# A hybrid decoder layer on one core: query blocks of three head groups multiplied in pairs by seven half products, attention's tasks ranked ahead, and the meta tokens' small copies moved from POOL to ACT

## The chip, the cores and the metric

The kernel runs on one core of a Trainium2 chip. The metric is the device time of one execution in microseconds (us); lower is better. Engines: PE multiplies matrices, DVE and ACT work on vectors and read and write SBUF and PSUM, POOL (GpSimd) does small vector work in SBUF, and SP starts the transfers. Every engine works through its own instructions in a fixed order.

## The reference, cut to what matters

A layer with two branches on the same normalised input `hn` (16 meta tokens and 512 tokens, 1024 wide), all in float32:

```python
proj = hn @ w_in.astype(h.dtype)
aq, ak, av, az, dq, dk, dv, dz, db, da, ga, gd = jnp.split(proj, offs, axis=-1)
o_a = diff_attention(qa, ka, va, lam)
y_a = (o_a * jax.nn.silu(az)) @ w_branch_attn.astype(h.dtype)
qkv = jnp.concatenate([dq, dk, dv], axis=-1)
qkv = jax.nn.silu(causal_depthwise_conv(qkv, conv_w))
o_d = gated_delta_chunked(pad_front(q), pad_front(k), pad_front(v), pad_front(beta), pad_front(g))
y_d = (o_d * jax.nn.silu(dz)) @ w_branch_delta.astype(h.dtype)
merged = jax.nn.sigmoid(ga) * y_a + jax.nn.sigmoid(gd) * y_d
return merged @ w_out.astype(h.dtype)
```

Attention has 8 heads with two softmax maps each, of which the second is subtracted with the weight `lam`. The delta rule has 8 heads of 128; its queries, keys and values (`dq`, `dk`, `dv`) pass a causal convolution over four tokens. It solves a triangular system in each chunk and carries a state from chunk to chunk. The output is normalised and the meta tokens are dropped.

## The kernel before, in words

**Blocks.** The columns of `w_in` are cut into blocks of 128, one per head and kind (`dq 3`, `av 5`). `dense_order` lists them in the order in which PE multiplies them. Heads go in four groups of two. In groups one to three the order is: both `dk`, both `dv`; then `ak av aq az` of the first attention head; both `dq`; one `dz`; `ak av aq az` of the second head; the other `dz`. Group nought has another order. The gate blocks `gd` and `ga` and the branches' products `yd` and `ya` come after the groups.

**Weights.** Each product is made in three passes: high part by high part, high by low, low by high (`PASSES`, the lists `hnH`, `hnL`, `wh`, `wl`). A raw block arrives by DMA in one of four buffers `raw`; ACT casts it to `wh`, and DVE writes `wl = raw - wh`. There are three buffers for such a pair of parts (`W`).

**Two ways to multiply.** `product` takes one block alone: 8 slices of the inner dimension by three passes, for each of two pieces of the tokens. For `dq` the pieces have 258 columns (`QSEG`; the first 12 tokens aren't needed). Its result goes by `conv_silu`, where ACT copies two pieces from PSUM into a buffer `xp`, into the convolution `conv`. `pair_of_blocks` multiplies two neighbouring blocks together. The two blocks, the two halves of the inner dimension and the two halves of the tokens (264 columns each) make eight half products; with sums of the weights (`split_pair`: four sums of 128x512 on DVE in `raw` and `st`, then four pairs of high and low parts, `wa`, `wb`, `wc` of 1024 columns and `wd` of 512) and sums of the tokens (`sumH`, `sumL`, made once) seven are enough. The parts of the result are put together afterwards: ACT copies the running sum three times (`snap`, `snap_c`, one of them into the single buffer `cn`), and DVE makes four totals of 128x264 straight into `xp` (or `vT` for attention). Then `whole_dk` or `whole_dv` runs the same `conv`. Before the change `dk` and `dv` of groups one to three and all `ak av` are multiplied in pairs.

**The order of the work** is made by a planner (`Plan`) when the kernel is built. Each task is a generator that yields the engine, the event or the buffer it wants next. At every step the planner takes the task that can begin first by its own cost figures; when several can begin at the same time, which on a busy engine is nearly always so, the lower `rank` goes first, and buffers are given out by rank too. Delta tasks have rank 0, the steps after a product rank 1, attention 2, the products 4. A helper emits all instructions, so that all have line 231 in the profile; they are told apart by their tiles.

**The delta rule of a group** (`delta_pair`): `keys` transposes the keys and `products` multiplies them; `queries` makes `qT` by `kT` and scales `qT`; the triangular recursion is 31 steps of two small DVE instructions on `tmps` and `ts`; `steps` then runs the chunks. The meta tokens are treated apart: the first 16 columns of the two heads' keys and values are copied into `km` and `vm` (POOL, a copy of 128x16 for each head), and PE transposes `km` and `vm`. In `meta_tokens` a power on POOL (`ms`) scales the transposed values to `vrm`.

**Attention** (`attention`, one task per head): scores into PSUM `psc`, the row maximum in `ast`, exponentials `e` on ACT; `combine` takes the reciprocal of a row sum, multiplies it by `nlam` and by `l0` to the scale of the second map, and puts the two maps together.

Of the kernel before, what the change touches and what calls it, by code (L numbers as in the profile page):

```python
# [21 lines left out]
NM = 16  # L22
# [34 lines left out]

ORDER = dense_order()

PAIRS = [n for n, (name, i) in enumerate(ORDER) if name == "ak" or name in ("dk", "dv") and i > 1 and i % 2 == 0]  # L60
PAIRED = {m for n in PAIRS for m in (n, n + 1)}
HALF = L // 2
PASSES = ((0, 0), (0, 1), (1, 0))
# [25 lines left out]
class Plan:  # L89
# [24 lines left out]
    def spawn(self, gen, rank=None):  # L114
        time, src = self.here() if self.task else (0.0, SP)
        self.tasks.append(Task(gen, self.task.rank if rank is None else rank, time, src))

    def done(self, event):
        self.events[event] = self.here()
# [146 lines left out]
def hybrid_block(ctx: ExitStack, tc: tile.TileContext, x, meta, wblk, wbd, wout, pcol, prow, out):  # L266
# [630 lines left out]
    def whole_dv(h, which):  # L897
        pair["v", h], _ = yield from conv(which, 16 + h, 0, None)
        done(f"dv{h}")

    def after_dq(h, banks):
        pair["q", h], _ = yield from conv_silu(banks, h, NM, "qT")
        give("y")
        done(f"dq{h}")
# [82 lines left out]
    def delta_pair(gi):  # L987
# [41 lines left out]
        def keys(i):  # L1029
            h = hs[i]  # L1030
            yield f"dk{h}"
            k = pair["k", h]

            def head():
                yield POOL
                G.tensor_copy(out=km[:, 16 * i:16 * i + 16], in_=k[:, 0:NM])
                tick(name("km"), 2)

            spawn(head())
            yield ("ktd",)  # L1040
            kd[i] = slot(dp, [P, NC, P], F32, "ktd")
            t4 = sc[:, i, :, :]
            yield ("pdl",)
            yield PE
            pt = bank("pdl").rearrange("p (c d) -> p c d", d=P)
            for c in range(NC):
                T.transpose(pt[:, c, :], k[:, chunk(c)], ident)
            for c in range(NC):
                yield ACT
                A.activation(out=mk(dp, [P, P], F32, "sqk", 1), in_=pt[:, c, :], func=AF.Square,  # L1050
                             accum_out=t4[:, c, kt_:kt_ + 1])

            def decayed():

                for c in range(NC):
                    yield ACT
                    A.activation(out=kd[i][:, c, :], in_=pt[:, c, :], func=AF.Copy, scale=edl[:, c, h:h + 1])
                give("pdl", pt)
                done(f"kd{h}")

            spawn(decayed())
            yield DVE
            V.tensor_scalar_add(out=t4[:, :, kt_], in0=t4[:, :, kt_], scalar1=4e-6)

            def root():
                yield DVE
                V.tensor_scalar_mul(out=t4[:, :, vs_], in0=t4[:, :, kt_], scalar1=0.25)
                yield POOL
                G.tensor_tensor(out=t4[:, :, vs_], in0=t4[:, :, vs_], in1=phalf[:, 0:4], op=ALU.pow)
                done(f"vs{h}")  # L1070

            spawn(root())
            yield DVE
            V.reciprocal(out=t4[:, :, s_], in_=t4[:, :, kt_])
            yield DVE
            V.tensor_tensor(out=t4[:, :, s_], in0=t4[:, :, s_], in1=beta[:, 0:4, h], op=ALU.mult)
            done(f"s{h}")

        def values(i):
            h = hs[i]  # L1080
            yield f"dv{h}"
            v = pair["v", h]
            yield POOL
            G.tensor_copy(out=vm[:, 16 * i:16 * i + 16], in_=v[:, 0:NM])
            tick(name("vm"), 2)
            yield ("vr",)
            vr[i] = slot(dp, [P, NC, P], F32, "vr")
            yield f"vs{h}"
            yield ("pdl",)
            yield PE  # L1090
            pt = bank("pdl").rearrange("p (c d) -> p c d", d=P)
            for c in range(NC):
                T.transpose(pt[:, c, :], v[:, chunk(c)], ident)
            give("y")
            for c in range(NC):
                yield ACT
                A.activation(out=vr[i][:, c, :], in_=pt[:, c, :], func=AF.Copy, scale=sc[:, i, c, vs_:vs_ + 1])
            give("pdl", pt)
            done(f"v{h}")
# [413 lines left out]
    def attention(h):  # L1513
# [11 lines left out]
        def combine(i, st, es):  # L1525
            N = NM + P * (i + 1)
            yield DVE
            V.reciprocal(out=st[:, 5:6], in_=st[:, 4:5])
            yield DVE
            V.scalar_tensor_tensor(out=st[:, 6:7], in0=st[:, 5:6], scalar=nlam, in1=l0[:, i:i + 1], op0=ALU.mult, op1=ALU.mult)  # L1530
            yield DVE
            V.scalar_tensor_tensor(out=es[0], in0=es[1], scalar=st[:, 6:7], in1=es[0], op0=ALU.mult, op1=ALU.add)
            give("e")

            yield ("pm",)
            which = plan.task.slot
            pm = late["pm"][which]
            yield ACT
            A.copy(out=pm[:, 0:2, 0:NM], in_=es[0][:, 0:NM].unsqueeze(1).broadcast_to([P, 2, NM]))
            yield DVE  # L1540
            V.tensor_tensor(out=pm[:, 2, 0:NM], in0=es[0][:, 0:NM], in1=pm[:, 0, 0:NM].bitcast(F32), op=ALU.subtract)
            yield ("pT",)
            pT, pmT = slot(ap, [P, NC, P], F32, "pT"), mk(ap, [96, P], F32R, "pmT", SLOTS["pT"])
            yield ("pat",)
            yield PE
            pt = bank("pat")
            for n in range(i + 1):
                T.transpose(pt[:, n * P:(n + 1) * P], es[0][:, chunk(n)], ident)
            give("e")
            w = (i + 1) * P  # L1550
            dst = pT[:, 0:i + 1, :].rearrange("p n q -> p (n q)")
            yield ACT
            A.copy(out=dst, in_=pt[:, :w])
            give("pat", pt)
            yield ("pat",)
            po = bank("pat")
            yield PE
            T.transpose(po[0:96, P:2 * P], pm.rearrange("p a t -> p (a t)").bitcast(F32), ident)
            plan.give("pm", which)
            yield ACT  # L1560
            A.copy(out=pmT, in_=po[0:96, P:2 * P])
            yield PE
            T.matmul(po[:, 0:P], pmT, late["vm"], start=True, stop=False)
            for n in range(i + 1):
                T.matmul(po[:, 0:P], pT[:, n, :], vs[:, n, :], start=False, stop=n == i)
            give("pT")
            yield ACT
            A.copy(out=o[:, i, :], in_=po[:, 0:P])
            A.activation(out=po[:, P:2 * P], in_=po[:, 0:P], func=AF.Square, accum_out=ss[:, i:i + 1])
            give("pat", po)  # L1570
            tick(f"ao{h}", NC)
# [71 lines left out]
    tails, highs, lows = dict(od=[None] * H, oa=[None] * H), {}, {}  # L1643

    AFTER = dict(dk=after_dk, dv=after_dv, dq=after_dq, aq=after_aq)
    WHOLE = dict(dk=whole_dk, dv=whole_dv, ak=whole_ak, av=whole_av)
    parts, th_, mg = {}, {}, {}

    def branch(name, of):
# [499 lines left out]
    for n, rank in ((1, 0), (0, 0.1), (2, 0.2), (3, 0.4), (4, 0.5)):  # L2149
        spawn(normalise(n), rank)  # L2150
    for h in range(H):
        spawn(attention(h), 2)
    plan.run()


# [44 lines left out]
```

## Time and profile before

| | before |
|---|---|
| median of 3 runs | 757.09 us (756.8 to 757.27) |
| the profiled execution's own time | 757.23 us |
| its span, first to last instruction | 755.5 us |
| PE busy | 734.0 us, 97% of the span |
| PEld busy (loading of weights into PE) | 666.7 us, 88% |
| DVE busy | 624.5 us, 83% |
| ACT busy | 495.8 us, 66% |
| POOL busy | 84.4 us, 11% |
| granted PE clock | 0.998 of full speed |

The profile is one execution. A group row gives an instruction's form, its count, busy time and mean duration in ns, then the idle time just before it and what ended that. A timeline row begins with the start and the duration in us; in square brackets stands the idle time before it and what released it. A row of waits gives the total, the number and the longest. Matmuls overlap, so the duration of one is longer than its share of PE's time.

### The profile page before, as it was taken

To read this page: it belongs to the slowest core of one execution; us is meant where nothing else is said; L and a number is where in the kernel's file an instruction comes from. 1 tells how busy PE (TensorE), PEld (TensorE's weight loads), DVE (VectorE), ACT (ScalarE), POOL (GpSimd) and SP (SyncE) were. 2 spreads that over 40 slices of the span, in tenths; PEclk is the share of its full clock that TensorE was granted. 3 is DMA by queue.
4 is the path that set the end of the run, shared out by engine and by line. 5 is a ranking of instruction groups with operands and counts; after the bars stand their busy time and mean duration, and the time that the engine had idled before them with its cause. 6 is when DMAs were issued, how large, how long until landed. Compare 5 with 4: busy or idle time off the path is not lost.

```text
span 755.5 us, 14375 instructions
## 1 busy us (share of the span) xinstructions
PE 734.0 (97%) x5311; PEld 666.7 (88%) x5311; DVE 624.5 (83%) x1431; ACT 495.8 (66%) x1306; POOL 84.4 (11%) x102
## 2 busy tenths in 40 slices
PE   4999999999999999999999999999999999999996
PEld 4998988989899899999889989988988998899875
DVE  6999999978899779989978989984697869797453
ACT  6369565869875778985587986767776445555132
POOL 3216000203000202200020300100100000000001
PEclk9999999999999999999999999999999999999999
DMA  8141322315304122531320441361023443132602
GB/s 307 52 135 33 111 82 66 92 29 155 113 29 153 18 70 85 168 85 43 120 65 29 150 138 37 125 184 58 29 83 113 142 130 121 56 119 90 240 4 108
DMA packets 45430, 74.86 MB, mean 99 GB/s; under 512 B 20728, under 2 KB 25636, under 8 KB 45360
## 3 DMA queue, kind: packets, MB, share of 16 engines
q1 hardware_dynamic: 45360, 73.95, 31.2%
q8 instruction: 41, 0.67, 0.4%
q14 instruction: 29, 0.24, 0.1%
HBM read 67.58 MB, written 6.36 MB: 98 GB/s over the span
## 4 chain that ended last, share of the span: by engine, by line
PE 81%; DVE 7%; ACT 5%; issue 2%; POOL 2%; DMA 1%; SPq 0%; POOLq 0%; ACTq 0%; DVEq 0%
PE bank L231 78%; PE psc L231 3%; DVE wl L231 2%; DVE y L231 1%; ACT wh L231 1%; POOL ms L231 1%; DMA xt<-in_x_dram 1%; ACT ak L231 1%; ACT sqk L231 0%; DVE aq L231 0%; DMA odd<-room 0%; ACT TM L231 0%; DVE room L231 0%; DVE hnL L231 0%; POOL ass L231 0%
## 5 line engine op out<-in xcount | busy, mean ns | idle before, releaser
L231 PE MATMUL bank<-hnH,wh 128*128 128x512 f32 (+4 forms) x664 | 232.7, 354 | 1.1 <-ACT hnH L231 0.8
L231 PE MATMUL bank<-hnH,wl 128*128 128x512 f32 (+4 forms) x664 | 221.6, 337 | 0.0
L231 PE MATMUL bank<-hnL,wh 128*128 128x512 f32 (+4 forms) x664 | 221.5, 337 | 0.0
L231 ACT CAST wh<-raw 128x1024 fp32r<-128x1024 f32 (+1 forms) x120 | 116.4, 971 | 48.8 <-PE bank L231 43.8
L231 DVE TENSOR_TENSOR wl<-raw,wh 128x1024 fp32r<-128x1024 f32 (+1 forms) x120 | 134.8, 1124 | 13.1 <-ACT wh L231 12.6
L231 PEld LDWEIGHTS bank<-hnH,wh 128*128 128x128 f32 x664 | 124.4, 189 | 14.7 <-ACT hnH L231 1.0
L231 PEld LDWEIGHTS bank<-hnH,wl 128*128 128x128 f32 x664 | 124.1, 188 | 14.0
L231 PEld LDWEIGHTS bank<-hnL,wh 128*128 128x128 f32 x664 | 124.4, 189 | 9.0
L231 PE MATMUL bank<-sumH,wh 128*128 128x264 f32 x224 | 67.3, 300 | 0.0
L231 PE MATMUL bank<-sumH,wl 128*128 128x264 f32 x224 | 63.5, 284 | 0.0
L231 PE MATMUL bank<-sumL,wh 128*128 128x264 f32 x224 | 63.5, 284 | 0.0
L231 DVE SCALAR_TENSOR_TENSOR y<-xp,pc,y 128x528 f32<-128x528 f32 (+1 forms) x72 | 54.5, 759 | 1.3 <-ACT y L231 1.2
L231 PEld LDWEIGHTS bank<-sumH,wh 128*128 128x128 f32 x224 | 42.3, 189 | 0.6 <-issue 0.2
L231 PEld LDWEIGHTS bank<-sumL,wh 128*128 128x128 f32 x224 | 42.3, 189 | 0.0
L231 PEld LDWEIGHTS bank<-sumH,wl 128*128 128x128 f32 x224 | 42.1, 188 | 0.0
L231 ACT ACTIVATE e<-psc,ast 128x144 f32<-128x144 f32 (+3 forms) x64 | 34.5, 541 | 8.7 <-DVE ast L231 8.2
L231 PE MATMUL bank<-btH,wh 128*128 128x256 f32 x128 | 36.2, 283 | 0.5 <-ACT sn L231 0.5
L231 PE MATMUL bank<-btH,wl 128*128 128x256 f32 x128 | 35.9, 280 | 0.0
L231 PE MATMUL bank<-btL,wh 128*128 128x256 f32 x128 | 35.9, 280 | 0.0
L231 ACT CAST wh<-st 128x1024 fp32r<-128x1024 f32 x22 | 23.1, 1048 | 16.2 <-PE bank L231 15.9
L231 POOL TENSOR_TENSOR ass<-ass,mhalf 128x4 f32<-128x4 f32 x8 | 8.7, 1084 | 222.8 <-DVE ass L231 163.4
L231 DVE TENSOR_TENSOR wl<-st,wh 128x1024 fp32r<-128x1024 f32 x22 | 27.8, 1266 | 2.4 <-ACT wh L231 2.3
(373 smaller groups left out, 1732.3 us busy)
## 6 DMA issues: line engine op xcount, KB each, us to landing
raw<-in_wblk_dram SPq DMA_DIRECT2D x96, 512.0 KB, 3.5
raw<-in_wout_dram SPq DMA_DIRECT2D x8, 512.0 KB, 4.9
xt<-in_x_dram SPq DMA_DIRECT2D x4, 512.0 KB, 6.2
TM<-gcd SPq DMA_DIRECT2D x8, 256.0 KB, 5.4
xr<-in_x_dram SPq DMA_DIRECT2D x8, 256.0 KB, 6.4
out_dram<-xr SPq DMA_DIRECT2D x8, 256.0 KB, 2.2
room<-scrm SPq DMA_DIRECT2D x12, 128.0 KB, 3.4
oad<-room SPq DMA_DIRECT2D x6, 256.0 KB, 3.8
```

Source lines behind the costliest of these rows:

```text
L231: return real(*args, **kw)
```

## The change

- `PAIRS` takes in `dq` of groups one to three: those six blocks are multiplied as three pairs by seven half products. A new function `whole_dq` runs the convolution on a finished block, as `whole_dk` does.
- The copies into `km` and `vm` go from POOL to ACT.
- The scale of attention's second map is made by a `tensor_scalar` with two column scalars on `l0`, where a `scalar_tensor_tensor` stood; the product is the same.
- Attention's tasks get rank 1 where they had 2.

```diff
-PAIRS = [n for n, (name, i) in enumerate(ORDER) if name == "ak" or name in ("dk", "dv") and i > 1 and i % 2 == 0]
+PAIRS = [n for n, (name, i) in enumerate(ORDER) if name == "ak" or name in ("dk", "dv", "dq") and i > 1 and i % 2 == 0]
...
+    def whole_dq(h, which):
+        pair["q", h], _ = yield from conv(which, h, NM, "qT")
+        give("y")
+        done(f"dq{h}")
...
-                yield POOL
-                G.tensor_copy(out=km[:, 16 * i:16 * i + 16], in_=k[:, 0:NM])
+                yield ACT
+                A.copy(out=km[:, 16 * i:16 * i + 16], in_=k[:, 0:NM])
...
-            yield POOL
-            G.tensor_copy(out=vm[:, 16 * i:16 * i + 16], in_=v[:, 0:NM])
+            yield ACT
+            A.copy(out=vm[:, 16 * i:16 * i + 16], in_=v[:, 0:NM])
...
-            V.scalar_tensor_tensor(out=st[:, 6:7], in0=st[:, 5:6], scalar=nlam, in1=l0[:, i:i + 1], op0=ALU.mult, op1=ALU.mult)
+            V.tensor_scalar(out=st[:, 6:7], in0=l0[:, i:i + 1], scalar1=st[:, 5:6], scalar2=nlam, op0=ALU.mult, op1=ALU.mult)
...
-    WHOLE = dict(dk=whole_dk, dv=whole_dv, ak=whole_ak, av=whole_av)
+    WHOLE = dict(dk=whole_dk, dv=whole_dv, dq=whole_dq, ak=whole_ak, av=whole_av)
...
-        spawn(attention(h), 2)
+        spawn(attention(h), 1)
```

In the instruction lists of the engines the change shows as follows. PE, group one, the query blocks before the change, where the first block's second piece ends and the second block's first piece begins (`wh_21` and `wl_22` are the first block's parts, `wh_23` and `wl_24` the second's):

```order
L231 MATMUL bank_5_82<-hnH,wh_21_118 128x258
L231 MATMUL bank_5_82<-hnL,wh_21_118 128x258
L231 MATMUL bank_5_82<-hnH,wl_22_119 128x258
L231 MATMUL bank_3_80<-hnH,wh_23_120 128x258
L231 MATMUL bank_3_80<-hnL,wh_23_120 128x258
L231 MATMUL bank_3_80<-hnH,wl_24_121 128x258
```

And after it, in the middle of the pair's seven products, where one half product with token sums ends and the next, with the same weights' other half, begins (`sumH`, `sumL` are the token sums' high and low parts):

```order
L231 MATMUL bank_4_81<-sumH_37_136,wh_23_120 128x264
L231 MATMUL bank_4_81<-sumL_41_140,wh_23_120 128x264
L231 MATMUL bank_4_81<-sumH_37_136,wl_24_121 128x264
L231 MATMUL bank_6_83<-sumH_34_133,wh_23_120 128x264
L231 MATMUL bank_6_83<-sumL_38_137,wh_23_120 128x264
L231 MATMUL bank_6_83<-sumH_34_133,wl_24_121 128x264
```

In each of the three groups 96 products of 258 columns become 84 of 264; PE has 36 products fewer in all, and nothing else is added to it or taken from it.

DVE, group one, before: the sums of the second attention pair (`st`, `raw`), and the first two instructions of the triangular recursion (`tmps`, `ts`) among them:

```order
L231 TENSOR_TENSOR st_115<-raw_14_111 128x512
L231 TENSOR_TENSOR st_115<-st_115,raw_16_113 128x512
L231 TENSOR_TENSOR wl_20_117<-raw_17_114,wh_19_116 128x1024
L231 TENSOR_TENSOR raw_14_111<-raw_16_113,raw_14_111 128x512
L231 TENSOR_TENSOR ak_2563<-vT_93_655,ak_2563 64x528
L231 SCALAR_TENSOR_TENSOR aq_2564<-bank_2_79,aq_2564 64x512
L231 TENSOR_TENSOR tmps_2602<-room_31_130,ts_1613 99x31
L231 SCALAR_TENSOR_TENSOR room_32_131<-room_33_132,bank_4_81 128x512
L231 TENSOR_TENSOR ts_1613<-ts_1613,tmps_2602 99x31
```

After, ahead of that place: the new sums of the query pair, among the low parts of other blocks and the meta tokens' scales (`ms`):

```order
L231 TENSOR_TENSOR st_115<-raw_15_112 128x512
L231 TENSOR_TENSOR wl_20_117<-raw_16_113,wh_19_116 128x1024
L231 TENSOR_TENSOR vT_93_655<-bank_6_83,vT_93_655 128x264
L231 TENSOR_TENSOR st_115<-st_115,raw_14_111 128x512
L231 TENSOR_TENSOR ms_952<-ms_952,medl 32x1
L231 TENSOR_TENSOR wl_22_119<-raw_14_111,wh_21_118 128x1024
L231 TENSOR_TENSOR raw_15_112<-raw_14_111,raw_15_112 128x512
L231 TENSOR_SCALAR ms_952<-blk_103,ms_952 32x2
L231 TENSOR_TENSOR raw_14_111<-raw_14_111,st_115 128x512
```

The query pair's four sums stand ahead of group one's recursion, whose first instruction now comes 37 rows behind the last of them; the sums of the second attention pair come behind that first instruction.

POOL, group nought, as a piece of the difference (`km` and `vm` are the meta tokens' columns, `ms` the power, `TM` the decay masks):

```order
-L231 COPY km_668<-kT_549 128x16
-L231 COPY km_668<-kT_604 128x16
-L231 COPY vm_669<-y_612 128x16
 L231 TENSOR_TENSOR sc_665<-sc_665,phalf 128x4 x2
 L231 TENSOR_TENSOR ms_670<-ms_670,phalf 32x1
-L231 AFFINE_SELECT TM_680<-TM_680 128x512
-L231 COPY vm_669<-y_797 128x16
-L231 AFFINE_SELECT TM_680<-TM_680 128x512
+L231 AFFINE_SELECT TM_680<-TM_680 128x512 x2
```

The four copies leave POOL's list; the last of them stood behind the power `ms` and a mask. On ACT that last copy now stands right behind the second of the four casts of token sums (`sumH`).

## The prediction

> **What bounds the kernel now.** I read the page first: its busy times, and the chain of work that ended last.
>
> ```profile
> span 755.5 us, 14375 instructions
> PE 734.0 (97%) x5311; PEld 666.7 (88%) x5311; DVE 624.5 (83%) x1431; ACT 495.8 (66%) x1306; POOL 84.4 (11%) x102
> PE 81%; DVE 7%; ACT 5%; issue 2%; POOL 2%; DMA 1%; SPq 0%; POOLq 0%; ACTq 0%; DVEq 0%
> ```
>
> PE is occupied for 734 of 755.5 us and carries 81% of the chain. So a product that PE no longer makes is worth its time, if the others keep PE fed. Second, PE's waits, longest first:
>
> ```profile
> PE bank L231 <- ACT st L231: 7.7, 1, 7.7
> PE bank L231 <- POOL vm L231: 1.7, 1, 1.7
> PE bank L231 <- DVE ss L231: 1.3, 2, 0.9
> PE bank L231 <- ACT hnH L231: 0.8, 1, 0.8
> PE bank L231 <- DVE tdmt L231: 0.6, 1, 0.6
> ```
>
> The first, third and fourth belong to the start, which the change does not touch. Behind the start only one wait is longer than 0.6 us: that for `vm` on POOL.
>
> Third, busy time by stage. The first three rows are the stretches from a group's query products to the end of its triangular recursion; the fourth is the stage from 125 to 500 us, in which the three changed groups lie; the last three come just ahead of the query products.
>
> ```profile
> 205.00:250.00 45.00, 45.00 (x315) 41.47 (x314) 43.51 (x127) 29.65 (x82) 1.01 (x1) 1.00 0.25 77
> 330.00:375.00 45.00, 44.72 (x316) 41.50 (x315) 43.83 (x127) 28.78 (x79) 1.58 (x1) 1.00 0.27 86
> 455.00:500.00 45.00, 45.00 (x320) 41.82 (x319) 43.64 (x128) 30.82 (x85) 2.20 (x3) 1.00 0.36 115
> 125.00:500.00 375.00, 372.09 (x2913) 343.21 (x2912) 331.34 (x830) 284.94 (x841) 49.77 (x62) 1.00 0.31 92
> ...
> 195.00:205.00 10.00, 10.00 (x66) 8.74 (x65) 7.48 (x19) 7.15 (x26) 0.00 (x0) 1.00 0.39 107
> 320.00:330.00 10.00, 10.00 (x61) 8.68 (x61) 6.38 (x18) 7.00 (x24) 0.00 (x0) 1.00 0.24 67
> 450.00:455.00 5.00, 5.00 (x34) 4.48 (x34) 2.09 (x5) 2.19 (x10) 0.00 (x0) 1.00 0.67 189
> ```
>
> The columns after the length are PE, PEld, DVE, ACT, POOL, the clock and DMA. From 125 to 500 us PE idles for 2.9 us. DVE, which writes the low parts of the weights, is idle for 1.5, 1.2 and 1.4 us of each 45 us stretch: 97% busy. Ahead of the query products it idles for 2.5, 3.6 and 2.9 us. So PE is the bound, and DVE is second just where the change adds work to it.
>
> How thin is the cover? In the timeline I looked for each low part's end on DVE and its first use on PE. It is thinnest at the attention query block that follows the group's second pair of attention blocks:
>
> ```profile
> 360.69 1.22 DVE L231 TENSOR_TENSOR wl<-raw,wh 128x1024 fp32r<-128x1024 f32 x1
> 485.53 1.22 DVE L231 TENSOR_TENSOR wl<-raw,wh 128x1024 fp32r<-128x1024 f32 x1
> ```
>
> ```profile
> 364.65 0.40 PE L231 MATMUL bank<-hnH,wl 128*128 128x512 f32 x1
> 489.17 0.39 PE L231 MATMUL bank<-hnH,wl 128*128 128x512 f32 x1
> ```
>
> The weights are ready at 361.91 and 486.75 and used at 364.65 and 489.17: 2.7 and 2.4 us ahead, 2.6 in the mean.
>
> **The change part by part: PE.** Two query blocks take 2 x 2 x 8 x 3 = 96 products of 258 columns now. As a pair they take 7 x 4 x 3 = 84 of 264 columns. The duration of one (0.28 us) is not its price, since the next starts earlier; I take start to start, from the first and last row of two unbroken stretches, of 39 and 56 products:
>
> ```profile
> 51.06 0.28 PE L231 MATMUL bank<-hnH,wh 128*128 128x258 f32 x1
> ...
> 55.61 0.28 PE L231 MATMUL bank<-hnH,wl 128*128 128x258 f32 x1
> ...
> 130.39 0.29 PE L231 MATMUL bank<-hnL,wh 128*128 128x264 f32 x1
> ...
> 137.06 0.28 PE L231 MATMUL bank<-sumH,wl 128*128 128x264 f32 x1
> ```
>
> (55.61 - 51.06) / 38 = 0.1197 us, and (137.06 - 130.39) / 55 = 0.1213 us. A pair saves 96 x 0.1197 - 84 x 0.1213 = 11.49 - 10.19 = 1.30 us, three pairs 3.9 us. The wider columns are paid in this; the seven half products remove an eighth of the products, not an eighth of the time.
>
> The Trainium skill (TensorE: Matmul & The Clock Gate, section "Wait — 56ns, not 53.3ns?") puts the step of a warm matmul at its columns over 2.4 GHz plus about 2.5 ns, which would be 110 and 112.5 ns here. The rows show 9 ns more for both, at a granted clock of 1.00. An estimate by the Trainium skill's figure: three pairs would save 3.3 us, and the sum would end 0.6 us later.
>
> **DVE and ACT.** A pair adds four sums of 128x512 on DVE, one low part of 128x1024 and one of 128x512, and four totals of 128x264. The scale of attention's second map takes another form.
>
> ```profile
> L231 DVE TENSOR_TENSOR wl<-st,wh 128x1024 fp32r<-128x1024 f32 x22 | 27.8, 1266 | 2.4 <-ACT wh L231 2.3
> L231 DVE TENSOR_TENSOR wl<-raw,wh 128x512 fp32r<-128x512 f32 x22 | 15.4, 699 | 3.3 <-ACT wh L231 3.3
> L231 DVE TENSOR_TENSOR st<-st,raw 128x512 f32<-128x512 f32 x22 | 15.1, 686 | 0.2
> L231 DVE TENSOR_TENSOR xp<-bank,xp 128x264 f32<-128x264 f32 x12 | 5.1, 425 | 0.3 <-PE bank L231 0.2
> L231 DVE SCALAR_TENSOR_TENSOR ast<-ast,nlam,l 128x1 f32<-128x1 f32 x32 | 7.4, 230 | 0.4
> L231 DVE TENSOR_SCALAR sc<-sc 128x4 f32<-128x4 f32 x24 | 3.8, 162 | 2.1 <-ACT sqk L231 2.0
> ```
>
> Durations: 4 x 0.686 + 1.266 + 0.699 + 4 x 0.425 = 6.41 us. They overlap: where one lasts 1.24 us, the next begins after 1.17:
>
> ```profile
> 64.88 1.24 DVE L231 TENSOR_TENSOR sumL<-room,sumH 128x1056 fp32r<-128x1056 f32 x1
> 66.05 1.21 DVE L231 TENSOR_TENSOR wl<-raw,wh 128x1024 fp32r<-128x1024 f32 x1
> ```
>
> Ten instructions at 0.07 less leave 5.7 us. The new form of the scale stands in no trace; its bounds are 230 ns (no gain) and the 162 ns of the nearest one-input row, which I take: eight per group give back 0.5 us. DVE has 5.2 us more per group, 15.6 us in all, where it idled for 375 - 331.3 = 43.7 us. What hides it: the idle time ahead of each stretch (3.0 us in the mean), that in the stretch (1.3) and the lead of 2.6; together 6.9. What is wanted: 5.2 and the 1.3 by which PE comes earlier; together 6.5. So it fits, narrowly, if the order puts the pair's sums ahead of the recursion. In group one it does: the four sums stand ahead of the recursion's first `tmps`. I allow 0.5 us of new PE waiting per group, between nothing and the 2.6 worked out under the rivals: 1.5 us in all. The sums also need both raw blocks where a low part needs one; whatever stands behind a waiting sum on DVE waits too, and that is within the same allowance.
>
> ACT, per pair, casts one and a half tiles more and changes four copies of 258 columns into two of 264 and one into `cn`; and it makes the 16 small copies.
>
> ```profile
> L231 ACT CAST wh<-st 128x1024 fp32r<-128x1024 f32 x22 | 23.1, 1048 | 16.2 <-PE bank L231 15.9 <-DVE st L231 0.2
> L231 ACT COPY cn<-bank 128x264 f32<-128x264 f32 x14 | 5.3, 378 | 4.3 <-PE bank L231 4.2
> L231 ACT CAST pm<-e 128x32 fp32r<-128x32 f32 x32 | 7.0, 218 | 10.0 <-DVE e L231 9.7
> ```
>
> About 1.5 x 1.05 - 0.38 = 1.2 us per pair and at most 16 x 0.22 = 3.5 us: 7 us, against 375 - 284.9 = 90 us in which ACT idles in that stage. Price on the path: nothing. But a small copy now stops ACT until DVE has written its source, with casts of `wh` queued behind it; that is a rival below.
>
> **The small copies and PE's longest wait.** In group nought PE waits for the copy of `vm`, which stands on POOL behind a power of 7.95 us:
>
> ```profile
> 61.61 7.95 POOL L231 TENSOR_TENSOR ms<-ms,phalf 32x1 f32<-32x1 f32 x1 [2.45 <-DVE ms L231]
> ...
> 70.12 0.19 POOL L231 COPY vm<-y 128x16 f32<-128x16 f32 x1
> ```
>
> ```profile
> 67.65 1.05 PE L231 MATMUL bank<-kT 128*128 128x128 f32 x8
> 70.36 0.28 PE L231 MATMUL bank<-ident,vm 128*32 128x128 f32 x1 [1.66 <-POOL vm L231]
> ```
>
> ```profile
> 67.45 1.05 ACT L231 CAST sumH<-room 128x1056 fp32r<-128x1056 f32 x1
> ```
>
> On ACT the copy stands right behind this cast, which ends at 68.5. Three small copies ahead of it make that about 69.2, its own 0.2 makes it 69.4, and PE, done at 68.7, still waits about 0.8 us. So some 0.8 of the 1.66 us goes; the bounds are nothing and 1.66. In the other groups PE never waits for POOL, so there the move removes nothing.
>
> **Attention's rank.** It changes who goes first on a busy DVE or ACT. PE's waits after the start are each 0.6 us or less apart from `vm`, so there is little to win; what is put back are the convolutions, whose results PE uses later. I price it at nothing.
>
> **Sum.** The profiled execution took 757.23 us, 1.7 of them outside its span of 755.5. 757.23 - 3.9 - 0.8 + 1.5 = 754.0. The median of the runs, 757.09, is 0.14 lower, so I forecast 753.9. A measurement of this kernel can tell about 0.2%, or 1.5 us: faster means below 755.6, slower above 758.6.
>
> **The rivals.**
>
> *DVE becomes the bound (slower).* If the pair's work falls into the 45 us stretches and nothing of it into the idle time ahead, 5.2 + 1.3 - 1.3 - 2.6 = 2.6 us per group is uncovered, and PE stands for it at the attention query block after the second attention pair: 7.8 us in all. 757.1 - 3.9 - 0.8 + 7.8 = 760.2. For it: 97% in three stretches, leads of 2.4 and 2.7 us. Against: the sums stand ahead of the recursion in group one, and much of DVE's idle time is waiting for PE, which shrinks when DVE runs late. The change gains nothing once new waits reach 4.7 us, and loses measurably from 6.2 us on.
>
> *The gain is eaten (no change).* ACT stops at its small copies. In the three last groups there are 12; if each delays a cast beyond its lead by 0.35 us, that is 4.2 us and the time 756.6. For it: ACT takes its queue in order. Against: the leads of 2.4 us and more, and a copy of 0.22 us.
>
> *More goes.* Attention ahead and lighter POOL and DVE queues also remove the waits left: all of `vm`, and half of the 2.9 us of idle PE between 125 and 500 us, with no new ones. 757.1 - 3.9 - 1.7 - 1.45 = 750.1; with only the `vm` wait and none of the new ones, 751.5. Against: added DVE work makes waits rather than takes them.
>
> **How the numbers follow.** The forecast, with new waits between 0 and 3.2 us (752.4 to 755.6), has 0.55; the eaten gain, 755.6 to 758.6, 0.20; DVE as the bound, above 758.6, 0.13; more, 749 to 752.4, 0.12. Faster is 0.55 + 0.12 = 0.67, same 0.20, slower 0.13. The range leaves out the slower case and the lower third of the last: 751.0 to 758.6.
>
> **What would show it.** Right: 36 fewer products on PE, 12 of them per pair; the wait for `vm` on POOL gone and a shorter one for ACT in its place; DVE busy for 14 to 16 us more; leads at the attention query blocks between 0 and 3 us; waits for `wl` or `xp` of some tenths. Wrong: PE waiting for DVE `wl` or ACT `wh` by 2 us or more per group; or the span unchanged while PE's idle time between 125 and 500 us has grown from 2.9 to 7 us.

## The result, and the profile after

| | before | after |
|---|---|---|
| median, side by side on one chip | 757.03 us (756.8 to 757.27, 4 runs) | 761.1 us (760.71 to 762.32, 4 runs) |
| ratio | | 1.0051, 95% interval 1.0039 to 1.0063 |
| profiled execution, span | 755.5 us | 759.0 us (own time 760.71) |
| DVE busy | 624.5 us | 639.9 us |
| ACT busy | 495.8 us | 502.6 us |

The change made the kernel 4 us slower, where 3 us faster was forecast. The page of after, its first lines and the chain of work that ended last:

```profile
span 759.0 us, 14311 instructions
PE 734.2 (97%) x5275; PEld 665.8 (88%) x5275; DVE 639.9 (84%) x1461; ACT 502.6 (66%) x1325; POOL 86.5 (11%) x86
PE 68%; DVE 15%; ACT 11%; issue 3%; POOL 1%; DMA 1%; SPq 0%; POOLq 0%; DVEq 0%; ACTq 0%
```

PE has its 36 products fewer (5311 to 5275) and is busy for as long as before: 734.2 us against 734.0. The span grew by 3.5 us, 0.2 of them in PE's busy time and 3.3 in its idle time. In the chain PE fell from 81% to 68%, and DVE and ACT rose from 12% to 26%: the end is now reached by way of their work. PE's waits behind 40 us, in total, times and longest:

```profile
PE bank L231 <- ACT pmT L231: 2.8, 4, 1.6
PE bank L231 <- DVE xp L231: 1.6, 1, 1.6
PE bank L231 <- DVE qT L231: 1.0, 2, 0.7
PE psc L231 <- ACT e L231: 0.9, 2, 0.7
PE bank L231 <- ACT ao L231: 0.8, 1, 0.8
```

The 1.7 us for `vm` on POOL are gone. In their place stand waits for attention's small steps on ACT (`pmT`, `e`, `ao`) and for a pair's total (`xp`) and the queries (`qT`) on DVE. All waits behind 40 us add up to 9.1 us, where before had 5.1. None of them is for a low part `wl`. The stages that the prediction showed, now in after (length, PE, PEld, DVE, ACT, POOL, clock, DMA):

```profile
205.00:250.00 45.00, 44.76 (x299) 40.73 (x298) 43.72 (x121) 29.47 (x73) 2.08 (x1) 1.00 0.32 103
330.00:375.00 45.00, 44.37 (x296) 40.41 (x297) 44.10 (x126) 28.42 (x70) 2.11 (x1) 1.00 0.32 105
455.00:500.00 45.00, 42.79 (x299) 39.46 (x298) 43.54 (x119) 30.40 (x78) 2.20 (x3) 1.00 0.45 146
125.00:500.00 375.00, 368.59 (x2860) 339.32 (x2859) 341.84 (x841) 288.85 (x845) 52.92 (x50) 1.00 0.30 92
```

Between 125 and 500 us PE idles for 6.4 us where it idled for 2.9. Where it was lost can be followed by a landmark, the first product of the attention query block behind the second attention pair, once in each group. Before had it at 238.28, 364.19 and 488.71 us. In after's timeline:

```profile
235.07 0.39 PE L231 MATMUL bank<-hnH,wh 128*128 128x512 f32 x1
361.65 0.39 PE L231 MATMUL bank<-hnH,wh 128*128 128x512 f32 x1
489.64 0.39 PE L231 MATMUL bank<-hnH,wh 128*128 128x512 f32 x1
```

After is 3.2 us ahead in group one, 2.5 ahead in group two, 0.9 behind in group three, and 3.5 behind at the end of the span. So it loses 0.7 us between the first two landmarks, where group two's query pair lies (327 to 342 us), 3.4 up to the third and 2.6 behind it. A landmark tells where PE is in the order of the blocks, not how many of the small products it has left for later, so these are rough. The two longest waits begin at 329 and 465 us. At the first, PE (first fence) needs `pmT` after twelve products, and ACT (second fence) makes it last of a row:

```profile
328.47 0.28 PE L231 MATMUL bank<-hnH,wl 128*128 128x264 f32 x1
330.39 0.33 PE L231 MATMUL bank<-vm,pmT 96*128 96x128 f32 x1 [1.64 <-ACT pmT L231]
```

```profile
326.98 1.05 ACT L231 CAST wh<-raw 128x1024 fp32r<-128x1024 f32 x1 [0.36 <-PE bank L231]
327.93 0.70 ACT L231 ACTIVATE e<-psc,ast 128x528 f32<-128x528 f32 x1
...
328.79 0.38 ACT L231 COPY xp<-bank 128x264 f32<-128x264 f32 x1
329.06 0.63 ACT L231 CAST ak<-vT 64x528 fp32r<-64x528 f32 x1
329.59 0.59 ACT L231 ACTIVATE aq<-bank 64x512 fp32r<-64x512 f32 x1
330.08 0.25 ACT L231 CAST pmT<-bank 96x128 fp32r<-96x128 f32 x1
```

At the second, inside group three's query pair, the last half product needs a PSUM bank that DVE reads for the pair's total. DVE could begin when ACT's copy into `cn` ended (464.86), but has a low part ahead of it:

```profile
464.85 0.28 PE L231 MATMUL bank<-sumH,wl 128*128 128x264 f32 x1
466.69 0.39 PE L231 MATMUL bank<-hnH,wh 128*128 128x264 f32 x1 [1.56 <-DVE xp L231]
```

```profile
464.95 1.22 DVE L231 TENSOR_TENSOR wl<-raw,wh 128x1024 fp32r<-128x1024 f32 x1
466.20 0.77 DVE L231 TENSOR_TENSOR xp<-bank,cn 128x264 f32<-128x264 f32 x2
```

Last, groups of after that answer to rows of before, on DVE:

```profile
L231 DVE TENSOR_TENSOR xp<-bank,xp 128x264 f32<-128x264 f32 x18 | 7.6, 425 | 3.0 <-PE bank L231 2.0 <-ACT e L231 0.9
L231 DVE TENSOR_SCALAR ast<-l,ast,nlam 128x1 f32<-128x1 f32 x32 | 8.6, 269 | 0.5
```

The small copies on ACT take 216 ns (`km`) and 195 ns (`vm`). The durations are as forecast but for the new form of the scale: 269 ns, above the 230 of the old form that were taken as its upper bound.

### The profile page after: what moved, and what is told of

It reads as the page before. It is cut to its first block, busy times and chain, and to the rows that moved or that the text cites. A ratio compares the mean times of both kernels' runs of the same rounds, so it can differ in the third digit from the quotient of the medians.

```text
span 759.0 us, 14311 instructions
## 1 busy us (share of the span) xinstructions
PE 734.2 (97%) x5275; PEld 665.8 (88%) x5275; DVE 639.9 (84%) x1461; ACT 502.6 (66%) x1325; POOL 86.5 (11%) x86
## 4 chain that ended last, share of the span: by engine, by line
PE 68%; DVE 15%; ACT 11%; issue 3%; POOL 1%; DMA 1%; SPq 0%; POOLq 0%; DVEq 0%; ACTq 0%
PE bank L231 65%; DVE wl L231 4%; PE psc L231 2%; ACT wh L231 2%; ACT TM L231 1%; DVE ast L231 1%; DVE tmps L231 1%; ACT ak L231 1%; DVE ts L231 1%; ACT e L231 1%; DVE y L231 1%; DMA xt<-in_x_dram 1%; DVE MT L231 1%; ACT MT L231 1%; ACT sqk L231 1%
## 5 line engine op out<-in xcount | busy, mean ns | idle before, releaser
L231 PE MATMUL bank<-hnH,wh 128*128 128x512 f32 (+4 forms) x604 | 215.4, 360 | 2.4 <-DVE xp L231 1.6
L231 PE MATMUL bank<-hnL,wh 128*128 128x512 f32 (+4 forms) x604 | 204.7, 343 | 0.0
L231 PE MATMUL bank<-hnH,wl 128*128 128x512 f32 (+4 forms) x604 | 204.7, 342 | 0.0
L231 PEld LDWEIGHTS bank<-hnH,wh 128*128 128x128 f32 x604 | 113.0, 189 | 15.7 <-DVE xp L231 1.8
L231 PEld LDWEIGHTS bank<-hnH,wl 128*128 128x128 f32 x604 | 112.8, 188 | 13.9
L231 PEld LDWEIGHTS bank<-hnL,wh 128*128 128x128 f32 x604 | 113.0, 189 | 9.8
L231 PE MATMUL bank<-sumH,wh 128*128 128x264 f32 x272 | 82.6, 304 | 0.2
L231 PE MATMUL bank<-sumL,wh 128*128 128x264 f32 x272 | 77.1, 284 | 0.0
L231 PE MATMUL bank<-sumH,wl 128*128 128x264 f32 x272 | 77.1, 284 | 0.0
L231 PEld LDWEIGHTS bank<-sumL,wh 128*128 128x128 f32 x272 | 51.4, 189 | 0.0
```

What stands on the lines that cost most here:

```text
L231: return real(*args, **kw)
```

## Experiments

Each time is the median of several runs beside the kernel before on the same chip, whose median lay between 757.08 and 757.22 us.

| run | what it is | us | ratio to before, 95% interval |
|---|---|---|---|
| e1 | changed kernel, rank 2 | 801.27 | 1.0573 (1.0551 to 1.0595) |
| e2 | before, rank 1 | 756.16 | 0.9983 (0.9974 to 0.9992) |
| e3 | before, three pairs | 802.02 | 1.0587 (1.0573 to 1.0602) |
| e4 | before, small copies and form | 779.05 | 1.0284 (1.0266 to 1.0301) |
| e5 | rank 1, three pairs | 760.39 | 1.0041 (1.0028 to 1.0054) |
| e6 | rank 1, small copies and form | 757.40 | 1.0003 (0.9994 to 1.0011) |
| e7 | changed kernel, pairs in groups one and three | 755.62 | 0.9982 (0.9973 to 0.9990) |
| e8 | changed kernel, pair in group two alone | 761.57 | 1.0053 (1.0037 to 1.0068) |
| e9 | after's order, the pairs' sums small | 760.26 | 1.0037 (1.0023 to 1.0051) |
| e10 | e9, their casts small too | 758.54 | 1.0020 (1.0011 to 1.0029) |
| e11 | rank 1, pairs in groups one and three | 754.72 | 0.9966 (0.9955 to 0.9978) |
| e12 | changed kernel, a planner figure +1 ns | 767.82 | 1.0139 (1.0125 to 1.0153) |
| e13 | e11 and the form | 756.90 | 1.0000 (0.9992 to 1.0009) |
| e14 | e5 and the form | 760.72 | 1.0045 (1.0034 to 1.0057) |
| e15 | e5, a planner figure +1 ns | 760.85 | 1.0058 (1.0042 to 1.0073) |
| e16 | changed kernel, a planner figure -2 ns | 760.49 | 1.0038 (1.0026 to 1.0050) |
| e17 | after, three instructions earlier | 762.77 | 1.0066 (1.0052 to 1.0080) |
| e18 | rank 1, pair in group two alone | 757.68 | 1.0006 (0.9998 to 1.0015) |

The first theories were: R, attention's rank makes PE wait for ACT; D, the pairs' work on DVE; A, the small copies on ACT; S, later O, the order that the planner makes of it all.

### The parts one by one (e1 to e4)

e1 undoes the rank alone, e2 makes it alone:

```diff
-        spawn(attention(h), 1)
+        spawn(attention(h), 2)
```

> The changed kernel with attention's tasks back at rank 2; query pairs, small copies by ACT and the new form of the scale stay. Theory R (the rank: attention's products come to PE just when their exponentials and transposes are written, so PE waits for ACT, as in the row of waits for pmT, 2.8 us in 4): the loss goes and the forecast's sum appears, 753 to 755 us, and the waits for pmT fall below 1 us in all. Theory D (the query pairs load DVE, whose totals xp and queries qT come late): nothing changes, 760 to 762 us, and PE's wait for xp stays. Theory A (small copies on ACT hold up what stands behind them): likewise 760 to 762 us. Theory S (no part has a price of its own; each shifts the order of the whole plan by a few us either way): anything from 755 to 762, and the sum of the single parts does not give the whole.

> The kernel before with attention's tasks at rank 1 and nothing else. Theory R: PE waits for pmT and e as in the changed kernel, with no saving beside it: 757.0 + 4.1 (the loss) + 3.9 (the saving that was to be had) is 765 at most, 760 at least. Theories D and A: 756 to 758 us. Theory S: within 3 us of 757, either way.

e3 is the kernel before with `dq` in `PAIRS` and `whole_dq`; e4 the kernel before with the lines on `km`, `vm` and the scale.

> The kernel before with the three query pairs and nothing else. Theory R: the saving of 3.9 us less the allowance of 1.5 appears, 753 to 755 us, and PE's waits for xp and qT stay below 0.5 us each. Theory D: 760 to 762 us, with the wait for xp of 1.6 us or more in it. Theory A: 753 to 755 us. Theory S: between 754 and 760 us.

> The kernel before with the copies into km and vm on ACT and the scale of the second map as tensor_scalar, and nothing else. Theories R and D: the wait of 1.7 us for vm on POOL goes, wholly or by half, 755.3 to 756.5 us. Theory A: ACT stops at its small copies, 759 to 762 us. Theory S: within 3 us of 757, either way. DVE is busy for some 2 us less if the new form takes 162 ns instead of 230, and for the same if it does not.

Measured: 801.27, 756.16, 802.02 and 779.05 us. e2 came out as theories D, A and S had it; e1, e3 and e4 missed every theory by far. Theory R is refuted: rank 1 alone gains 1 us, and undoing it in the changed kernel costs 40. At rank 2, the pairs or the small copies, each alone, cost 45 and 22 us; beside each other, with rank 1, they cost 4. Edits whose own work is a few microseconds had the planner make another order, and a bad one. Not all of it is waiting: in e1 PE's granted clock is 0.970 in the mean, with 0.50 for some 44 us in all while PE works, and the same 5275 products keep PE busy for 751.3 us instead of 734.2. Of e4, PE's rows at its longest wait, and of e1 PE's two dearest waits behind the start and a stretch:

```profile
235.33 1.11 PE L231 MATMUL bank<-vs,pT 128*128 128x128 f32 x8
236.27 0.71 PE L231 MATMUL bank<-ident,vT 128*16 128x128 f32 x5
240.86 0.39 PE L231 MATMUL bank<-hnH,wh 128*128 128x264 f32 x1 [3.88 <-DVE vT L231]
```

```profile
PE bank L231 <- DVE qT L231: 11.7, 6, 3.2
...
PE bank L231 <- ACT vT L231: 5.7, 1, 5.7
```

```profile
225.00:250.00 25.00, 16.70 (x105) 14.98 (x104) 21.19 (x68) 11.51 (x37) 2.55 (x4) 0.81 0.26 91
```

In e4 the values of the second group's first head are transposed (`ident,vT`) at 236 us, right behind that attention's last `vs,pT`; in e6, the same parts at rank 1, at 210 to 212. Attention has one buffer each for `vs`, `aq` and `ak`, and two for `vT`. I read from this that an attention task put behind the convolutions keeps `vs`, the next head's values keep `vT`, the pair of blocks behind them can't write its total, its bank stays taken and PE stops. That reading is argued from the trace; a second buffer for `vs` was not tried. What the runs show is that rank 1 is worth 40.2 us with all parts (e1 against after), 41.6 with the pairs (e3, e5) and 21.7 with the small copies (e4, e6), and 1 us with neither.

### At rank 1: which part costs (e5 to e8, e18)

e5 is e2 with the three pairs; e6 the changed kernel without them; e7, e8 and e18 pair some groups only, as in

```diff
+PAIRS = [... name in ("dk", "dv") and i > 1 or name == "dq" and i in (2, 6) ...]
```

> The changed kernel with the copies of km and vm on POOL and the scale of the second map in its old form: rank 1 and the query pairs alone. Theory D (at rank 1 it is the pairs that cost: the work of a pair on DVE delays what PE needs next): 760 to 763 us, as the changed kernel or with the 1.7 us for vm on top. Theory A (the small copies on ACT cost): the loss of some 5 us against rank 1 alone goes, 754 to 757 us. Theory O (the order that the planner makes from all parts together costs; each set of parts makes another order): between 755 and 762 us, and PE's longest waits stand at other places than 328 and 465 us.

> The changed kernel without the query pairs: rank 1, small copies by ACT, the new form of the scale. Theory D: 754.5 to 756.5 us, rank 1 alone or 1 us better. Theory A: 759 to 762 us. Theory O: 755 to 760 us, and with the run of the pairs alone at rank 1 the two differences from rank 1 alone do not add up to the changed kernel's 5 us.

> The changed kernel with the query blocks of groups one and three in pairs and those of group two one by one. Theory D with the same price in each group: two thirds of the way from the kernel without pairs (e6) to the changed kernel (761). Theory O, with the loss at one place: the wait of 1.8 us at 328 us, just ahead of group two's query blocks, and the one of 1.7 us at 465 belong to orders that come with group two's pair; without it the saving of two pairs shows, 2.6 us less than the kernel without pairs: 753 to 755 us.

> The changed kernel with the query blocks of group two alone in a pair. Theory D with the same price in each group: one third of the way from e6 to 761. Theory O with the loss at group two: as far from e6 as the changed kernel plus 2.6 us, 760 us or more; or, if only the three together make that order, the saving of one pair, 1.3 us below e6.

> The kernel before with attention's tasks at rank 1 and the query blocks of group two alone in a pair. If group two's pair costs 4 to 5 us whatever stands beside it: 759.5 to 761.5 us, against 756.2 for rank 1 alone. If it cost so only beside the small copies or the other pairs: 754.5 to 757.5 us.

Measured: 760.39, 757.40, 755.62, 761.57 (758.93 to 763.47) and 757.68 us. Two pairs, in groups one and three, gain 1.8 us beside the small copies (e6 to e7) and 1.4 without (e2 to e11): 0.7 to 0.9 each. Group two's pair costs 1.5 (e2 to e18), 4.2 (e6 to e8), 5.7 (e11 to e5) and 5.5 us (e7 to after), so it loses in all four comparisons. The 4.2 needs care: e8's six executions spread over 4.5 us and had granted clocks from 0.998 to 0.991, in the main the longer the lower; the one with 0.998 took 758.93, 1.5 above e6's median. At a clock as in the other runs, then, group two's pair costs about 1.5 us without the two other pairs and 5.5 to 5.7 beside them. e18 fell between its two expectations. Theory D with one price for each group falls, and so does theory A: without the small copies the three pairs still take 760.4. The copies and the form together cost 1.2 (e2 to e6), 0.9 (e11 to e7) and 0.7 us (e5 to after; within the two intervals); beside group two's pair alone 3.9 (e18 to e8), or 1.3 with e8's execution at 0.998. Over e2, the pairs add 4.2 us (e5), the copies and the form 1.2 (e6), both 4.9 (after): at rank 1 these parts nearly add up, against theory O's expectation.

e7 and after run alike up to 310 us; e7 then passes the landmarks of groups two and three, in its timeline, at

```profile
363.11 0.39 PE L231 MATMUL bank<-hnH,wh 128*128 128x512 f32 x1
...
485.80 0.48 PE L231 MATMUL bank<-hnH,wh 128*128 128x512 f32 x1
```

At the first it is 1.5 us behind after, at the second 3.8 ahead. Is it that ACT is full where group two's pair begins? In the ten microseconds of the first long wait, e7 and then after:

```profile
325.00:335.00 10.00, 10.00 (x79) 9.54 (x78) 8.52 (x16) 9.54 (x19) 0.00 (x0) 1.00 0.35 100
```

```profile
325.00:335.00 10.00, 8.36 (x67) 7.96 (x66) 7.70 (x15) 9.43 (x23) 0.00 (x0) 1.00 0.32 98
```

ACT is 95% busy in e7 and 94% in after; PE never stops in e7 and stops for 1.64 us in after. A block taken alone needs no copy by ACT while it is multiplied. In a pair, PE comes to steps that need ACT's copies of the running sum (e17 below shows such a wait), and a half product takes only 12 x 0.121 = 1.45 us. But a full ACT is not enough as the cause. Group one's pair begins in after at 201.9 us beside an ACT that is as full, and PE idles for 0.37 us there:

```profile
200.00:210.00 10.00, 9.63 (x73) 8.90 (x72) 7.83 (x14) 9.49 (x24) 0.00 (x0) 1.00 0.36 102
```

And in e18 group two's pair, from 331.5 to 343.4 us, meets an ACT that is 60% busy, and still costs 1.5 us. PE's idle time in e18 stands later, in waits for the delta rule's chunks; in e5 too (e18 in the first fence, e5 in the second):

```profile
330.00:340.00 10.00, 9.69 (x76) 9.42 (x76) 8.13 (x22) 6.00 (x17) 0.00 (x0) 1.00 0.55 175
345.00:430.00 85.00, 83.88 (x677) 76.87 (x676) 80.55 (x201) 59.83 (x180) 8.76 (x12) 1.00 0.22 67
```

```profile
345.00:430.00 85.00, 82.00 (x660) 75.03 (x659) 77.68 (x194) 59.20 (x177) 10.10 (x12) 1.00 0.22 67
```

From 345 to 430 us PE idles for 1.1 us in e18 and 3.0 in e5, for nothing in e2 and e11, and for 0.1 in after. So group two's pair costs in each of these orders, but at another place in each. Why it is this pair, the runs do not show.

### The same order with less work (e9, e10)

The pairs' four sums on DVE, and in e10 the casts of their high parts on ACT, take 8 columns, while the planner is charged for all, so that every engine's list stays as in after:

```diff
+                if tiny:
+                    plan.spend(DVE, 504 / 0.96)
+                    out, in0, in1 = out[:, 0:8], in0[:, 0:8], in1[:, 0:8]
```

> The changed kernel with the same order of instructions on every engine, but the four sums of each query pair's weights on DVE take 8 columns instead of 512 (the planner is charged for 512). It leaves out 504 of 512 columns of those sums, so the queries of groups one to three are not those of the reference. DVE has some 12 x 0.6 = 7 us less to do. Theory D (DVE's time for the sums is what PE pays for): the 5 us above the kernel with pairs in groups one and three go, 755 to 757 us. Theory O (the order itself: PE stands behind ACT's and DVE's steps for attention at a few places): 759.5 to 761.5 us, with PE's waits of 1.6 us for pmT and for xp still there.

> As the run before, and the casts of the query pairs' high parts on ACT take 8 columns too (the planner is charged for all); so the high parts are left out as well. ACT has some 3 x 3.3 = 10 us less to do. If the pair's added time on DVE and ACT together is what costs: 754 to 756 us. Theory O: 758.5 to 761 us, the waits behind attention's casts remaining.

Measured: 760.26 and 758.54 us, 0.8 and 2.6 below after; the intervals of e9 and of after overlap, those of e10 and after don't. The busy times of e9 and e10, and PE's two long waits in e10:

```profile
PE 734.1 (97%) x5275; PEld 666.0 (88%) x5275; DVE 633.6 (84%) x1461; ACT 503.1 (66%) x1325; POOL 80.6 (11%) x86
```

```profile
PE 732.5 (97%) x5275; PEld 665.3 (88%) x5275; DVE 634.4 (84%) x1461; ACT 494.5 (65%) x1325; POOL 80.4 (11%) x86
```

```profile
PE bank L231 <- ACT pmT L231: 2.2, 2, 1.6
PE bank L231 <- DVE xp L231: 1.5, 1, 1.5
```

The long waits stand as they did in after, in e9 too. DVE is busy for 6.3 us less in e9, of the 15.4 that the change added; ACT in e10 for 8.1 us less than in after, more than the 6.8 that the change added. So ACT's work in the pairs has a price: taking it out saves 1.7 us more. Nearly all of that is PE's busy time, 1.6 us less for the same products in the same order. A product's row lasts 0.28 us and the next begins after 0.12, so a delay of up to 0.16 us between two products shows as busy and not as a wait; such delays may be what went, which was not taken apart. With most of ACT's and part of DVE's work gone, the kernel is still 3 us slower than with two pairs.

### The same parts in another order (e12, e14 to e16)

e12 and e16 are the changed kernel with one figure of the planner altered, 95 and 92 for 94; no instruction differs but in its place:

```diff
-            return (51 if op == "copy" and psum else 94) + n / 1.2 + ...
+            return (51 if op == "copy" and psum else 95) + n / 1.2 + ...
```

> The changed kernel with one figure of the planner altered, by which an ACT instruction that does not copy from PSUM is taken to last 1 ns longer. No instruction is added, removed or resized; the planner may only put them in another order. Theories D and A (the parts of the change have their prices): 760 to 762 us. Theory O: another order and another time, more than 2 us away from 761, either way.

> The changed kernel with the planner's figure for ACT lowered by 2 ns, no instruction added, removed or resized. If group two's pair costs by itself: 760 to 762 us. If the order costs: more than 1.5 us away from 761, either way.

e14 is e5 with the new form of the scale; e15 is e5 with DVE's figure 70 for 69.

> The changed kernel with the small copies on POOL: rank 1, all three query pairs, the new form of the scale. If group two's pair costs by itself: 759.5 to 761.5 us, as with the pairs alone (760.4). If the order costs: more than 1.5 us away from 760.4, either way, and PE's longest waits at other places.

> Rank 1 and all three query pairs (the run of 760.4 us), and one figure of the planner altered: a DVE instruction is taken to last 1 ns longer. If group two's pair costs by itself: 759.5 to 761.5 us. If the order costs: more than 1.5 us away, either way; the best that could come is the time of the fastest version less the saving of one more pair, 754.7 - 1.3 = 753.4 us.

Measured: 767.82 (e12), 760.49 (e16), 760.72 (e14) and 760.85 us (e15). The orders of e15 and e16 give part of the output other than the reference has it, which the edits did not intend, so their times count with that reserve. One nanosecond in a figure made 6.7 us, more than the whole change; e12's waits are in the delta rule's chunks:

```profile
PE bank L231 <- DVE vin L231: 2.0, 3, 1.0
PE bank L231 <- DVE S L231: 1.5, 3, 0.9
```

So the order is worth several microseconds by itself, as theory O has it. But the three others came back to within 0.7 us of after, and of six orders with all three pairs at rank 1 none has a median below 760.3. That speaks for a cost that goes with group two's pair, which the order may add to. It is not proof that no order avoids it: e16's five executions had granted clocks of 0.993 to 0.996, and its trace has 3.4 us at 0.50 from 261.9 us on, behind waits of 0.81 and 0.39. As an estimate, half of the 3.4 us is lost there, so that the traced execution of 759.4 us would have taken 757.7 at the full clock.

### The waits themselves (e17)

e17 has after's lists, and puts three instructions ahead of their places: ACT's copies into `pmT` and `cn`, and DVE's total behind the latter. In the code they are issued where their input is ready, and the planner is charged for them at the old place:

```diff
+            if early:
+                nc.scalar.copy(out=pmT, in_=po[0:96, P:2 * P])
             yield ACT
-            A.copy(out=pmT, in_=po[0:96, P:2 * P])
```

> The changed kernel with the same instructions in the same order on every engine, but for three: on ACT the copy into pmT for which PE waits at 328 us stands five places earlier, ahead of a cast of weights, an exponential, a copy and two steps of the next head's keys and queries; on ACT the copy into cn at 464 us two places earlier; on DVE the total that reads it four places earlier, ahead of a low part of weights. If these two places are what the change lost: the waits of 1.6 us each go to 0.3 or less and the time falls by 2.5 to 3.3 us, to 758 or 758.5. If the time is lost all along and only shows there: 760.5 to 761.5 us, with other waits in their place.

Measured: 762.77 us, 1.7 above after and above both expectations. Both waits are gone. Others stand in their place, on PE, with ACT's rows at the first of them and PE's clock around it:

```profile
336.47 0.39 PE L231 MATMUL bank<-sumH,wh 128*128 128x264 f32 x1 [2.17 <-ACT xp L231]
...
480.80 0.38 PE L231 MATMUL bank<-qT,kT 128*128 128x128 f32 x1 [1.48 <-DVE qT L231]
```

```profile
333.34 1.07 ACT L231 CAST ak<-ak 64x1056 fp32r<-64x1056 f32 x1
334.43 0.62 ACT L231 CAST wh<-raw 128x512 fp32r<-128x512 f32 x1
335.07 1.07 ACT L231 CAST ak<-ak 64x1056 fp32r<-64x1056 f32 x1
336.05 0.37 ACT L231 COPY xp<-bank 128x264 f32<-128x264 f32 x1
```

```profile
334.20:337.50 3.30, 1.12 (x10) 1.03 (x9) 3.10 (x12) 3.24 (x6) 0.00 (x0) 1.00 0.12 34
337.50:340.90 3.40, 3.40 (x18) 3.39 (x17) 3.33 (x8) 1.20 (x4) 0.00 (x0) 0.50 0.34 129
```

PE came to the pair's fifth half product 1.5 us sooner and stood there, since ACT copies the running sum into `xp` behind two of attention's casts. The clock explains why e17 is slower than after: behind the wait it is 0.50 for 3.4 us, and PE makes 18 products there, against 30 in the 3.4 us that follow. Two of the five executions had a granted clock of 0.999 and took 761.57 and 761.89 us; the three longer ones had 0.995 to 0.997. So taking out both waits gained nothing, and a new, longer wait cost a drop of the clock besides. I read from this that the two long waits of after were a place where the loss showed, not its cause: ACT is behind there, and PE meets it at a later step.

### The fastest version (e11, e13)

> The kernel before with attention's tasks at rank 1 and the query blocks of groups one and three in pairs, and nothing else: small copies on POOL, old form of the scale. If the gains add (rank 1 alone 1.1 us below before, two pairs 1.8 us below the kernel without pairs): 754 to 755 us, the fastest so far. Theory O in its strong form (each set of parts draws its own order, nothing adds): anything from 754 to 760 us.

> The fastest version so far (rank 1, query pairs in groups one and three) with the new form of the scale of the second map. The form has no price on the path: 754 to 755.5 us if the order stays near the same; more than 756.5 if the order that comes with it is worse.

Measured: 754.72 and 756.90 us. The gains of e2 and of two pairs add, and e11 beats both kernels: 0.9966 (0.9955 to 0.9978) of before. Its longest wait behind the start:

```profile
PE bank L231 <- POOL vm L231: 1.7, 1, 1.7
```

It still waits for `vm`; no other wait of its is longer than 0.5 us. The form of the scale, with 32 x 0.046 = 1.5 us more of DVE (269 ns against 223 in e11), cost 2.2 us there (e11 to e13) and 0.3 beside three pairs (e5 to e14). The copies on ACT, added to e13, take 1.3 us back (e7).

## Why the prediction was wrong

**The first step that failed: PE's saving of 3.9 us.** The price of a product was read rightly, in unbroken stretches. But PE's busy time, which was to fall by 3.9 us, went from 734.0 to 734.2: 4.1 us of the 6.7 by which the traced execution missed the sum (760.71 against 754.0). Where the saving went is open. The first passes with token sums take 304 ns in the mean where they took 300, and delays of up to 0.16 us between products count as busy. Groups one and three gave 0.7 to 0.9 us for a pair, near the 1.3 - 0.5 = 0.8 of the sum, but by luck: from e2 to e11 PE's busy time fell by 1.2 us, where two pairs were to save 2.6, and its idle time did not grow, where 1.0 was allowed. The Trainium skill's step (TensorE: Matmul & The Clock Gate, section "Wait — 56ns, not 53.3ns?") gave an estimate of 3.3 us for three pairs instead of 3.9. The prediction's rows measure 9 to 10 ns more for a product than that step, and no run's time tells 3.3 from 3.9.

**DVE's load** came out as forecast in total, by two errors that cancel: 14 to 16 us more were expected, 15.4 are there. The new form, which was to give back 1.5 us, takes 1.2 more (8.6 against 7.4), so the pairs' part is smaller than the 17 us reckoned. The price of the new form was outside its bounds: 269 ns against 162 taken and 230 as the upper end.

**The second: "I allow 0.5 us of new PE waiting per group".** The waits behind 40 us grew by 4.0 us although the 1.7 for `vm` went, so 5.7 new ones can be read off by name, where 1.5 were allowed. PE's whole idle time grew by 3.3 us, where the sum had 0.7.

**The step under it: "Price on the path: nothing" for ACT.** It set 7 us of ACT's work against 90 us of idle time in a stage of 375. With 8.6 us of ACT's work taken out and the order kept (e9 to e10), the time fell by 1.7 us, so that work does reach PE. The forecast looked for the thinnest cover at the low parts, with leads of 2.4 us and more, and never asked how long PE can wait for the copies and totals in the middle of a pair. That this is why group two's pair loses is argued only: where it begins ACT is 94% busy, but it is 95% busy where group one's pair begins.

**"Attention's rank ... I price it at nothing"** was right for the kernel before (1 us) and wrong for this change: at rank 2 the rest of it costs 44 us, about 17 of them PE's slower products. It stood on the waits of the old order, and a planner's order doesn't outlive the edit.

**The wait for `vm`** went wholly, not by half; yet the small copies and the form made the kernel 0.7 to 1.2 us slower at rank 1, and more beside group two's pair alone.

**The rivals.** *DVE becomes the bound* gave 760.2, within 1 us of the result, but for a reason that didn't hold: PE waits for no low part, and with 6.3 us of DVE's work gone (e9) the time fell by 0.8, which is within the intervals. *The gain is eaten* by ACT's stops at small copies is refuted by e5. That an edit's order could cost or gain several microseconds by itself, as e12 and e1 to e4 show, was not among them.

**What stays open:** why it is group two's pair that loses, and how much of its 1.5 to 5.7 us belongs to the pair and how much to the orders in which it was seen.

## What to carry to other kernels

Reckon a forecast in the critical engine's busy time and its idle time apart, and look at both afterwards: here the saving was missing in the busy time, where no list of waits shows it. Try a change place by place: two of the three pairs gain 1.8 us together, and the third loses 5.5 beside them. Where a greedy planner sets the order, alter one of its figures by a nanosecond first: the spread that this makes (7 us here) is what any single edit's result has to be read against. Removing the longest wait by hand tests whether it is a cause: here a longer one came 6 us later.

## What the runs showed of the hardware

- A DVE `tensor_scalar` on 128x1 with two column scalars takes 269 ns, where `scalar_tensor_tensor` with one took 223 to 230 and a `tensor_scalar` on 128x4 of another kind 162.
- PE's granted clock was 0.50 for 3.4 us at a time behind some waits: in e17 behind one of 2.17 us, in e16 behind 1.4 us of idle time in 3.5. In after it stayed at 1.00 behind waits of 1.64 and 1.56 us, so the length of a wait does not settle it alone. At 0.50 a product of 264 columns came every 0.22 us (e17, rows from 337.5 us on) instead of every 0.12.
- In the 25 us of e1 in which PE idles for 8.3, the clock was 0.81 in the mean. In the whole of e1 the same 5275 products kept PE busy for 751.3 us instead of 734.2, so about 17 of its 40 us go with the clock.
